# First weights in eight steps with the rows of x, four columns side by side, and squares of two rows at once

## The chip, the cores and the metric

The kernel runs on one core of one Trainium2 chip. The metric is the device time of one execution in microseconds (us), lower is better. Before the change the median of 3 runs is 984.67 us (984.04 to 986.51).

## What is computed

Two layers of a decoder trunk on 256 tokens of width 1024, in float32. Each layer is a half-weighted SwiGLU feed-forward, a token mixer, a cross-attention to a memory of 256 tokens, and a second feed-forward; every part reads an RMS-normed x. What matters here is the very first part:

```python
def rmsnorm(x, g):
    x32 = x.astype(jnp.float32)
    y = x32 * lax.rsqrt(jnp.mean(x32 * x32, axis=-1, keepdims=True) + EPS)
    return y.astype(x.dtype) * g

def swiglu(x, w_gate, w_up, w_down):
    return (jax.nn.silu(x @ w_gate) * (x @ w_up)) @ w_down

x = x + 0.5 * swiglu(rmsnorm(x, ffn1_norm[l]), ffn1_w_gate[l], ffn1_w_up[l], ffn1_w_down[l])
```

w_gate and w_up are 1024 x 2816, w_down 2816 x 1024. The mixer of the first layer needs a bias per head, looked up in a small table (rel_bias), and one sink per head (ev_sinks).

## The kernel before, in words

x lies with its 1024 features on the partitions, as 8 row blocks (KT = 8) of 128 features x 256 tokens. Weights are cut into tiles of 128x128; the host lays the 2768 tiles out in the order in which they are used. `Stream` (line 51) loads them in chunks of 16 tiles (1 MB) through SP's queue into four buffers `raw`, and splits them in blocks of 8 tiles (`fill`, line 87): ScalarE rounds a block to a high part `whi` (line 99), VectorE takes the rest as a low part `wlo` (line 100). x is split alike, with the gain of the norm multiplied in (`normed_tile`, line 263: ScalarE line 267, VectorE line 268). A product of one tile with one row block, a pair in what follows, is two matmuls (`mm`, line 319): whi against both parts of x, 512 columns (line 322), and wlo against the high part, 256 columns (line 323).

The scale of the norm (one over the root mean square) is not needed for the products, only when their sums are evacuated. `squares` (line 272) sums the squares of x over the row blocks, on GpSimd for the first seven (lines 275, 279, 280), on ScalarE and VectorE for the last (lines 282, 283); `norm_scale` (line 285) has TensorE sum over partitions (line 291), GpSimd take the power, and TensorE spread the result (line 301).

The work around the change is the start. Lines 221 to 226 issue the first loads: vecs (all gains) on ScalarE's queue, and on SP's queue, in turn, five pieces of x and five pieces of the first two chunks, then the third chunk. Lines 236 to 240 warm up TensorE with WARM = 9 matmuls of the identity matrix, which GpSimd makes first. Lines 896 to 899 split x and the first 32 tiles, and `gates` (line 405) multiplies three columns of w_gate side by side, so that each row block of x that arrives gives work to three accumulators (24 tiles in all); then the columns follow one by one (`gate_up`, line 416). A gate or up sum is joined out of PSUM into a buffer `w1` (eight of them) by line 332 on ScalarE and line 333 on VectorE, and waits there for the norm's scale.

`make_bias` (line 717) loads the bias table, the sinks (one row repeated over 128 partitions, line 723) and a one-hot matrix with three DMAs on GpSimd's queue.

TensorE's program follows `Order`: a list of work items, each with a cost, and tasks that fall due at a time on the list's own clock (`pe.after(delay, fn, cost)`); the squares' sum over partitions is due at 2300 of that clock, behind `gates`. The order of the instructions on each engine is then set at build time by a list scheduler; an engine runs its list in order.

Of the kernel before, what the change touches and what calls it, by code (L numbers as in the profile page):

```python
# [31 lines left out]
NEG = -1e30  # L32
BUCKETS = 32
# [15 lines left out]


class Stream:


# [4 lines left out]

    def __init__(self, nc, pool, src):
        self.nc, self.pool, self.src = nc, pool, src  # L60
        self.order = []
        self.raw, self.split = {}, {}
        self.n_loaded = self.n_split = 0
        self.due = deque()
        self.n_due = 0
        self.fine = False

    def load(self, cuts=(0, CHUNK)):

        c = self.n_loaded  # L70
        t = self.raw[c] = self.pool.tile([P, CHUNK * P], F32, name="raw", bufs=4)
        self.n_loaded += 1
        for i, j in zip(cuts, cuts[1:]):
            self.nc.sync.dma_start(t[:, i * P:j * P], self.src[c][:, i * P:j * P])
            yield

    def _load_to(self, n):
        while self.n_loaded < min(n, NTILES // CHUNK):
            for _ in self.load():
                pass  # L80

# [4 lines left out]

    def fill(self, cuts=None):
        if not self.due:
            return
        cuts = cuts or ((0, BLK // 2, BLK) if self.fine else (0, BLK))  # L90
        b = self.due.popleft()
        c, o = divmod(b * BLK, CHUNK)
        self._load_to(c + 1)
        raw = self.raw[c][:, o * P:(o + BLK) * P]
        hi = self.pool.tile([P, BLK * P], F32R, name="whi", bufs=self.BUFS)
        lo = self.pool.tile([P, BLK * P], F32R, name="wlo", bufs=self.BUFS)
        for i, j in zip(cuts, cuts[1:]):
            at = slice(i * P, j * P)
            self.nc.scalar.activation(hi[:, at], raw[:, at], AF.Copy)  # L99
            self.nc.vector.tensor_tensor(lo[:, at], raw[:, at], hi[:, at].bitcast(F32), op=ALU.subtract)  # L100
# [91 lines left out]
def build(nc, tc, ctx, a):  # L192
    consts = ctx.enter_context(tc.tile_pool(name="consts", bufs=1))
    wpool = ctx.enter_context(tc.tile_pool(name="wpool", bufs=1))
    act = ctx.enter_context(tc.tile_pool(name="act", bufs=1))
# [3 lines left out]
    def acc_tile():  # L199
        return psum.tile([P, 512], F32, name="acc", bufs=4)  # L200
# [10 lines left out]
    def w2():  # L211
        return act.tile([P, 512], F32, name="w2", bufs=6)
# [19 lines left out]
    mhalf = consts.tile([P, 2], F32, name="mhalf")  # L232
    nc.gpsimd.memset(mhalf, -0.5)


    warm = act.tile([P, 2], F32, name="ms", bufs=2)
    nc.scalar.activation(warm, mhalf, AF.Silu)
# [25 lines left out]
    def normed_tile(n, k, src):  # L263

        g = col(n.key, k)
        n.x[k] = x2 = Split(act.tile([P, 2 * S], F32R, name=n.name, bufs=n.n_bufs))
        nc.scalar.activation(x2.hi, halves(src), AF.Copy, scale=g)
        nc.vector.scalar_tensor_tensor(x2.lo, halves(src), g, x2.hi.bitcast(F32), op0=ALU.mult, op1=ALU.subtract)  # L268
        if not n.ready:
# [131 lines left out]
    def ffn(which, layer, n, nxt, first=False, last=False):  # L401
# [3 lines left out]
        def gates():  # L405

            for f in range(3):
                cur[f, 0] = acc_tile()
            for k in range(KT):
                for f in range(3):  # L410
                    w = ws.take(f"{which}_w_gate", layer, k * P, f * P)
                    mm(cur[f, 0], w, n.x[k], k == 0, k == KT - 1)
            for f in range(3):
                cur[f, 0] = join(w1(), cur[f, 0])
# [41 lines left out]
        def down_tok():  # L456
# [32 lines left out]
            def evac_tok(u, at, ps):  # L489
# [227 lines left out]
    def make_bias():  # L717

        tab = consts.tile([BUCKETS + 1, 8], F32, name="tab")
        nc.gpsimd.dma_start(tab[:BUCKETS], a["rel_bias"])  # L720
        nc.gpsimd.memset(tab[BUCKETS:BUCKETS + 1], NEG)
        sinks = consts.tile([P, 8], F32, name="sinks")
        nc.gpsimd.dma_start(sinks, bass.AP(tensor=a["ev_sinks"].tensor, offset=a["ev_sinks"].offset, ap=[[0, P], [1, 8]]))
# [11 lines left out]
        return sinks  # L735

# [276 lines left out]
```

## Time and profile before

| | us |
|---|---|
| median of 3 runs | 984.67 |
| lowest, highest | 984.04, 986.51 |
| profiled execution, its own time | 984.22 |
| its span in the trace | 982.4 |
| TensorE busy in the span | 968.7 (99%) |
| VectorE, ScalarE, GpSimd busy | 757.3, 580.6, 146.9 |

How to read it: times within the trace are us from the start of the span. PE is TensorE's matmuls, PEld its weight loads, DVE VectorE, ACT ScalarE, POOL GpSimd, SP the engine that issues most DMAs; a q behind an engine's name is its instruction queue. Matmuls overlap, so two rows of PE may run at one time, and the busy times of rows that overlap are not added up. Behind a row, in brackets, stands the time that the engine was idle before it and what ended that idle time. The profiled execution took 1.8 us more than its span.

### The profile page before, as it was taken

What the parts mean: (1) busy time and instruction counts of PE and PEld (TensorE: products, weight loads), DVE (VectorE), ACT (ScalarE), POOL (GpSimd) and SP (SyncE); (2) the same over time, 40 slices, a digit from 0 to 9 for tenths busy, and PEclk for the clock granted to TensorE, in tenths of its full rate; (3) what the DMA queues carried; (4) which work ended last, traced back from release to release, by engine and by line L of the source; (5) the groups of instructions that cost most, each with busy time, mean ns of one, the idle gap of its engine ahead of it and who ended that gap; (6) DMA issues with size and microseconds to landing.
All of it is one profiled execution on the core that took longest, in us unless ns stands there. A gap on an engine that the chain in (4) does not pass through costs nothing.

```text
span 982.4 us, 16594 instructions
## 1 busy us (share of the span) xinstructions
PE 968.7 (99%) x6442; PEld 902.3 (92%) x6442; DVE 757.3 (77%) x1284; ACT 580.6 (59%) x1026; POOL 146.9 (15%) x160
## 2 busy tenths in 40 slices
PE   7999999999999999999999999999999999999997
PEld 6899999999999999999999999999999999999896
DVE  6888877799876988877778878777668678887653
ACT  6665654575556666664556666555665657666542
POOL 6104003201241400002210000121005050000010
PEclk9999999999999999999999999999999999999999
DMA  9796655556463465565555565566545526555531
GB/s 308 256 343 236 225 187 209 172 215 214 171 212 133 171 211 188 201 214 189 198 204 190 205 214 186 201 212 217 179 154 187 181 95 219 210 199 192 209 129 44
DMA packets 28415, 193.66 MB, mean 197 GB/s; under 512 B 3346, under 2 KB 3730, under 8 KB 5808
## 3 DMA queue, kind: packets, MB, share of 16 engines
q1 hardware_dynamic: 26928, 186.66, 54.7%
q0 software_dynamic: 976, 5.37, 1.7%
q8 instruction: 50, 0.82, 0.3%
q10 hardware_dynamic: 432, 0.57, 0.2%
q14 instruction: 29, 0.24, 0.1%
HBM read 191.51 MB, written 4.22 MB: 199 GB/s over the span
## 4 chain that ended last, share of the span: by engine, by line
PE 97%; DMA 1%; SPq 0%; ACT 0%; DVE 0%; issue 0%; POOLq 0%; DVEq 0%
PE acc L322 41%; PE acc L323 21%; PE acc L327 7%; PE acc L329 7%; PE acc L328 7%; PE acc L481 1%; PE acc L482 1%; PE acc L480 1%; PE acc L370 1%; PE acc L371 1%; PE acc L372 1%; DMA raw<-in_w 1%; PE tr L587 1%; PE sc L571 1%; PE tr L579 1%; PE sc L480 0%
## 5 line engine op out<-in xcount | busy, mean ns | idle before, releaser
L100 DVE TENSOR_TENSOR wlo<-raw,whi 128x1024 fp32r<-128x1024 f32 (+2 forms) x356 | 435.1, 1225 | 150.8 <-ACT whi L99 147.9
L99 ACT ACTIVATE whi<-raw 128x1024 fp32r<-128x1024 f32 (+2 forms) x356 | 366.4, 1033 | 297.6 <-PE acc L322 137.0
L322 PE MATMUL acc<-x,whi 128*128 128x512 f32 x1408 | 462.7, 383 | 2.7 <-DVE x L268 2.7
L323 PE MATMUL acc<-x,wlo 128*128 128x256 f32 x1408 | 382.8, 273 | 0.5 <-DVE wlo L100 0.5
L322 PEld LDWEIGHTS acc<-x,whi 128*128 128x128 f32 x1408 | 265.9, 189 | 40.3 <-DVE x L268 3.3
L323 PEld LDWEIGHTS acc<-x,wlo 128*128 128x128 f32 x1408 | 269.9, 192 | 1.9 <-DVE wlo L100 1.5
L322 PE MATMUL acc<-h,whi 128*128 128x512 f32 x462 | 151.3, 382 | 0.0
L323 PE MATMUL acc<-h,wlo 128*128 128x256 f32 x462 | 125.4, 273 | 0.0
L322 PEld LDWEIGHTS acc<-h,whi 128*128 128x128 f32 x462 | 87.1, 189 | 12.0
L323 PEld LDWEIGHTS acc<-h,wlo 128*128 128x128 f32 x462 | 88.7, 192 | 0.2
L328 PE MATMUL acc<-h,whi 128*128 128x256 f32 x322 | 88.3, 278 | 0.0
L329 PE MATMUL acc<-h,wlo 128*128 128x256 f32 x322 | 87.5, 276 | 0.0
L327 PE MATMUL acc<-h,whi 128*128 128x256 f32 x322 | 86.3, 279 | 0.9 <-ACT h L386 0.9
L329 PE MATMUL acc<-x,wlo 128*128 128x256 f32 x304 | 84.6, 280 | 0.0
L328 PE MATMUL acc<-x,whi 128*128 128x256 f32 x304 | 83.5, 276 | 0.0
L327 PE MATMUL acc<-x,whi 128*128 128x256 f32 x304 | 82.7, 278 | 0.0
L333 DVE TENSOR_TENSOR w<-acc,w 128x256 f32<-128x256 f32 x197 | 82.2, 418 | 0.3
L332 ACT ACTIVATE w<-acc 128x256 f32<-128x256 f32 x197 | 72.6, 369 | 3.8 <-PE acc L323 3.8
L275 POOL TENSOR_TENSOR sqacc<-x 128x256 f32<-128x256 f32 x8 | 4.9, 615 | 421.4 <-DVE x L381 421.4
L279 POOL TENSOR_TENSOR sq<-x 128x256 f32<-128x256 f32 x48 | 53.1, 1112 | 89.5 <-DVE x L381 69.9
L327 PEld LDWEIGHTS acc<-h,whi 128*128 128x128 f32 x322 | 60.3, 192 | 2.0 <-ACT h L386 1.8
L329 PEld LDWEIGHTS acc<-h,wlo 128*128 128x128 f32 x322 | 61.7, 192 | 0.1
(179 smaller groups left out, 1207.1 us busy)
## 6 DMA issues: line engine op xcount, KB each, us to landing
raw<-in_w SPq DMA_DIRECT2D x171, 1024.0 KB, 5.0
dists<-line POOLq DMA_DIRECT2D x2, 1536.0 KB, 12.6
raw<-in_memT SPq DMA_DIRECT2D x3, 1024.0 KB, 4.9
bias<-dists POOLq DMA_DIRECT2D x2, 1024.0 KB, 10.1
raw<-in_w SPq DMA_DIRECT2D x2, 512.0 KB, 8.6
x<-in_xT SPq DMA_DIRECT2D x3, 256.0 KB, 8.3
kT<-in_final_norm SPq DMA_DIRECT2D x1, 512.0 KB, 3.7
out<-bias ACTq DMA_DIRECT2D x2, 256.0 KB, 2.7
```

The source lines that it names most:

```text
L99: self.nc.scalar.activation(hi[:, at], raw[:, at], AF.Copy)
L100: self.nc.vector.tensor_tensor(lo[:, at], raw[:, at], hi[:, at].bitcast(F32), op=ALU.subtract)
L279: nc.gpsimd.tensor_tensor(sq, src, src, op=ALU.mult)
L322: nc.tensor.matmul(ps, w[0], x2.both, start=start, stop=False)
L323: nc.tensor.matmul(ps[:, :S], w[1], x2.high, start=False, stop=stop)
L327: nc.tensor.matmul(ps[:, :S], w[0], x2.high, start=start, stop=False)
L328: nc.tensor.matmul(ps[:, :S], w[0], x2.low, start=False, stop=False)
L329: nc.tensor.matmul(ps[:, :S], w[1], x2.high, start=False, stop=stop)
L332: nc.scalar.activation(halves(out), unpaired(ps[:, S:]), AF.Copy)
L333: nc.vector.tensor_tensor(halves(out), unpaired(ps[:, :S]), halves(out), op=ALU.add)
L370: nc.tensor.matmul(ps[t], xh, wh, start=k == 0, stop=False)
L371: nc.tensor.matmul(ps[t], xh, wl, start=False, stop=False)
```

## The change

The first 32 tiles (FIRST = KT * SIDE, four columns of w_gate) leave the stream of 1 MB chunks. The host packs each row block of x with the four tiles that meet it into one row of 768 columns (`w0`, 8 x 128 x 768, 393 KB each), and SP loads these eight rows first, the first two of them in two pieces; two rows share one of the four `raw` buffers. The first norm reads x from these rows. Only the later work needs the tile x itself: it is loaded whole (1 MB) afterwards, and a GpSimd copy of one column makes that load wait for the fourth row's block. The squares leave the loop: ScalarE squares two row blocks at a time, from the tile x, GpSimd adds the four results, VectorE adds the two halves. They are due at 12000 of the order's clock and the sum over partitions at 18200. The warm-up uses a zero tile that VectorE clears, and 8 matmuls in place of 9. The bias table and the sinks become columns of vecs (84 to 100 columns), so that two of GpSimd's DMAs go; the load of the one-hot matrix is made to wait for x.

```diff
-WARM = 9
+WARM = 8
+SIDE = 4
+FIRST = KT * SIDE
+STEP = S + SIDE * P
-NVEC = VCOL["conv"] + 3 * 4
+VCOL["table"] = VCOL["conv"] + 3 * 4
+VCOL["sinks"] = VCOL["table"] + 8
+NVEC = VCOL["sinks"] + 8
...
+    def load_first(self):
+        rows = []
+        for k in range(KT):
+            if k % 2 == 0:
+                t = self.raw[k // 2] = self._raw()
+            o = k % 2 * STEP
+            cuts = {0: (0, S + P, STEP), 1: (0, S, STEP)}.get(k, (0, STEP))
+            for i, j in zip(cuts, cuts[1:]):
+                self.nc.sync.dma_start(t[:, o + i:o + j], self.first[k][:, i:j])
+            rows.append(t[:, o:o + S])
+        return rows
...
-    ws = Stream(nc, wpool, a["w"])
+    warm = consts.tile([P, P], F32, name="warm")
+    nc.vector.memset(warm, 0.0)
+    ws = Stream(nc, wpool, a["w0"], a["w"])
     nc.scalar.dma_start(vecs, a["vecs"])
-    pieces = chain(ws.load((0, 3, 9, CHUNK)), ws.load((0, 8, CHUNK)))
-    for k, n in ((0, 1), (1, 1), (2, 2), (4, 2), (6, 2)):
-        nc.sync.dma_start(x[:, k:k + n], a["xT"][:, k:k + n])
-        next(pieces)
-    ws._load_to(ws.AHEAD_CHUNKS)
+    first_rows = ws.load_first()
+    ws._load_to(ws.n_loaded + 1)
...
-        nc.tensor.matmul(pt[:, :P], ident, ident, start=True, stop=True)
+        nc.tensor.matmul(pt[:, :P], warm, warm, start=True, stop=True)
...
+    def squares_of_x(n):
+        two = None
+        for k in range(0, KT, 2):
+            sq = w2()
+            nc.scalar.activation(sq, x[:, k:k + 2].rearrange("p k s -> p (k s)"), AF.Square)
+            if two is None:
+                two = sq
+            else:
+                nc.gpsimd.tensor_tensor(two, two, sq, op=ALU.add)
+        n.acc = act.tile([P, S], F32, name="sqacc", bufs=2)
+        nc.vector.tensor_tensor(n.acc, two[:, :S], two[:, S:], op=ALU.add)
...
-            for f in range(3):
-                cur[f, 0] = acc_tile()
+            for f in range(SIDE):
+                cur[f, 0] = (acc_tile if f < SIDE // 2 else sc_tile)()
...
-        norm_scale(n)
+        if first:
+            pe.after(12000, lambda: squares_of_x(n), 0)
+        norm_scale(n, 18200 if first else 2300)
...
-        tab = consts.tile([BUCKETS + 1, 8], F32, name="tab")
-        nc.gpsimd.dma_start(tab[:BUCKETS], a["rel_bias"])
-        nc.gpsimd.memset(tab[BUCKETS:BUCKETS + 1], NEG)
-        sinks = consts.tile([P, 8], F32, name="sinks")
-        nc.gpsimd.dma_start(sinks, bass.AP(tensor=a["ev_sinks"].tensor, offset=a["ev_sinks"].offset, ap=[[0, P], [1, 8]]))
         oh = act.tile([BUCKETS + 1, 768], F32, name="bias", bufs=1)
+        nc.gpsimd.tensor_copy(oh[:, :1], x[:BUCKETS + 1, 0, :1])
         nc.gpsimd.dma_start(oh, a["onehot"])
...
+    n.acc = False
     for k in range(KT):
-        normed_tile(n, k, x[:, k])
+        normed_tile(n, k, first_rows[k])
         if k % 2 == 0:
-            ws.fill(((0, 3, 6, BLK), (0, 1, 4, BLK), (0, BLK), (0, BLK))[k // 2])
+            block = ws.begin()
+        cuts = (0, 1, SIDE) if k == 0 else (0, SIDE)
+        for i, j in zip(cuts, cuts[1:]):
+            ws.piece(block, k % 2 * SIDE + i, k % 2 * SIDE + j)
+        if k == KT // 2 - 1:
+            nc.gpsimd.tensor_copy(x[:, 0, :1], block[1][:, :1].bitcast(F32))
+            nc.sync.dma_start(x, a["xT"])
+    ws._load_to(ws.n_loaded + 1)
```

## Rows read from the trace of the kernel before

**Rows 1.** The waits of TensorE over the whole span: who waited for whom, us in total, times, the longest.
```profile
PE acc L322 <- DVE x L268: 2.7, 3, 1.3
PE tr L240 <- POOL ident masks.py:199: 2.5, 1, 2.5
PE acc L327 <- ACT h L386: 0.9, 2, 0.5
PE acc L323 <- DVE wlo L100: 0.5, 1, 0.5
```

**Rows 2.** TensorE's matmuls in order of time, the first 22 us: start, us, engine, line, operation, out<-in, count, and in brackets the idle time before.
```profile
2.54 4.21 PE L240 MATMUL tr<-ident 128*128 128x128 f32 x18 [2.54 <-POOL ident masks.py:199]
6.40 1.28 PE L322 MATMUL acc<-x,whi 128*128 128x512 f32 x3
7.85 0.81 PE L322 MATMUL acc<-x,whi 128*128 128x512 f32 x3
...
10.30 0.48 PE L322 MATMUL acc<-x,whi 128*128 128x512 f32 x1 [1.31 <-DVE x L268]
...
13.96 0.48 PE L322 MATMUL acc<-x,whi 128*128 128x512 f32 x1 [1.17 <-DVE x L268]
...
19.32 0.38 PE L322 MATMUL acc<-x,whi 128*128 128x512 f32 x1
19.68 0.38 PE L323 MATMUL acc<-x,wlo 128*128 128x256 f32 x1
19.89 0.38 PE L322 MATMUL acc<-x,whi 128*128 128x512 f32 x1
20.11 0.27 PE L323 MATMUL acc<-x,wlo 128*128 128x256 f32 x1
...
21.86 0.38 PE L322 MATMUL acc<-x,whi 128*128 128x512 f32 x1
22.07 0.50 PE L291 MATMUL tr<-ones,sqacc 128*128 128x1 f32 x4
```

**Rows 3.** Stretches of the start: from:to and length, busy us (and instructions) of PE, PEld, DVE, ACT and POOL, granted TensorE clock, mean busy share of the 16 DMA engines, GB/s.
```profile
2.00:3.40 1.40, 0.86 (x4) 0.86 (x5) 0.00 (x0) 0.68 (x2) 1.25 (x5) 1.00 0.93 240
3.40:5.50 2.10, 2.10 (x12) 2.10 (x12) 1.06 (x2) 1.30 (x3) 1.45 (x5) 1.00 0.74 272
5.50:7.60 2.10, 2.10 (x10) 1.96 (x10) 1.39 (x3) 1.04 (x4) 0.22 (x1) 1.00 1.05 175
7.60:10.00 2.40, 1.39 (x10) 1.12 (x8) 0.97 (x4) 0.89 (x3) 0.73 (x2) 1.00 0.98 331
10.00:13.00 3.00, 2.48 (x12) 1.80 (x12) 2.80 (x4) 2.09 (x5) 2.92 (x4) 1.00 1.05 393
```

**Rows 4.** DMA queues from 5.5 to 7.6 us: packets, MB, share of the 16 engines' time. q0 carries GpSimd's DMAs, q1 SP's.
```profile
q0 software_dynamic: 28, 0.00, 53.3%
q1 hardware_dynamic: 168, 0.36, 51.3%
```

**Rows 5.** GpSimd's list in order of time, the issues of its DMAs among it.
```profile
2.59 0.60 POOL L723 DMA_DIRECT2D sinks<-in_ev_sinks  x1
...
17.63 2.58 POOL L280 TENSOR_TENSOR sqacc<-sqacc,sq 128x256 f32<-128x256 f32 x2
```

**Rows 6.** DMA issues of the first 30 us: size of each, median us from issue to landing.
```profile
raw<-in_w SPq DMA_DIRECT2D x2, 512.0 KB, 8.6
x<-in_xT SPq DMA_DIRECT2D x3, 256.0 KB, 8.3
...
vecs<-in_vecs ACTq DMA_DIRECT2D x1, 42.0 KB, 2.6
...
sinks<-in_ev_sinks POOLq DMA_DIRECT2D x1, 4.0 KB, 6.2
```

**Rows 7.** The instructions that write or read the row blocks of x and the sum of squares: count, ns shortest/median/longest, first and last start.
```profile
L267 ACT ACTIVATE x<-x,vecs x8: 492/494/510, 3.4 to 14.6; 128x256 fp32r<-128x256 f32 x8
L268 DVE SCALAR_TENSOR_TENSOR x<-x,vecs x8: 473/829/953, 4.0 to 17.1; 128x256 fp32r<-128x256 f32 x8
L280 POOL TENSOR_TENSOR sqacc<-sqacc,sq x6: 794/910/1595, 9.8 to 18.6; 128x256 f32<-128x256 f32 x6
```

**Rows 8.** Groups of the first 22 us by line and shape: count, busy us, mean ns of one, idle time before.
```profile
L99 ACT ACTIVATE whi<-raw 128x512 fp32r<-128x512 f32 x1 | 0.6, 621 | 0.0
L99 ACT ACTIVATE whi<-raw 128x128 fp32r<-128x128 f32 x1 | 0.3, 292 | 0.0
L100 DVE TENSOR_TENSOR wlo<-raw,whi 128x512 fp32r<-128x512 f32 x1 | 1.1, 1096 | 0.0
L283 DVE TENSOR_TENSOR sqacc<-sqacc,sq 128x256 f32<-128x256 f32 x1 | 0.4, 427 | 0.6 <-POOL sqacc L280 0.6
masks.py:197 POOL MEMSET ident<- 128x128 f32 x1 | 0.2, 205 | 0.3 <-POOLq L979 0.3
```

**Rows 9.** Groups between 20 and 60 us by line and shape, columns as in rows 8.
```profile
L100 DVE TENSOR_TENSOR wlo<-raw,whi 128x1024 fp32r<-128x1024 f32 x18 | 21.7, 1221 | 4.1 <-ACT whi L99 4.0
L99 ACT ACTIVATE whi<-raw 128x1024 fp32r<-128x1024 f32 x18 | 18.9, 1061 | 10.4 <-PE acc L322 5.9 <-issue 2.6 <-ACT h L386 1.9
L332 ACT ACTIVATE w<-acc 128x256 f32<-128x256 f32 x16 | 5.8, 372 | 0.0
```

**Rows 10.** ScalarE in order of time, the first 22 us.
```profile
3.41 0.51 ACT L267 ACTIVATE x<-x,vecs 128x256 fp32r<-128x256 f32 x1 [0.72 <-DMA vecs<-in_vecs]
4.71 0.52 ACT L99 ACTIVATE whi<-raw 128x384 fp32r<-128x384 f32 x1 [0.79 <-DMA raw<-in_w]
```

More of the change, by code (lines that the diff above doesn't have):

```diff
@@ L57, with __init__ @@
     BUFS = 5
-    def __init__(self, nc, pool, src):
-        self.nc, self.pool, self.src = nc, pool, src
+    def __init__(self, nc, pool, first, src):
+        self.nc, self.pool, self.first, self.src = nc, pool, first, src
         self.order = []
         self.raw, self.split = {}, {}
-        self.n_loaded = self.n_split = 0
+        self.n_loaded = FIRST // BLK
+        self.n_split = 0
         self.due = deque()
@@ L66, in __init__, with _raw, chunk_of @@
         self.fine = False
[L68 to L75, printed above, removed]
-    def _load_to(self, n):
-        while self.n_loaded < min(n, NTILES // CHUNK):
-            for _ in self.load():
-                pass
+    def _raw(self):
+        return self.pool.tile([P, CHUNK * P], F32, name="raw", bufs=4)
+    def load_first(self):
[9 more added lines that the diff above has]
+        return rows
+    def chunk_of(self, b):
+        if b * BLK < FIRST:
+            return b, (S, STEP + S)
+        c, o = divmod(b * BLK - FIRST, CHUNK)
+        return FIRST // BLK + c, (o * P, (o + BLK // 2) * P)
+    def _load_to(self, n):
+        while self.n_loaded < min(n, FIRST // BLK + (NTILES - FIRST) // CHUNK):
+            c = self.n_loaded
+            t = self.raw[c] = self._raw()
+            self.nc.sync.dma_start(t, self.src[c - FIRST // BLK])
+            self.n_loaded += 1
     def _due_to(self, n):
@@ L85, in _due_to, with begin @@
             self.n_due += 1
[L87 to L90, printed above, removed]
+    def begin(self):
         b = self.due.popleft()
-        c, o = divmod(b * BLK, CHUNK)
+        c, (left, right) = self.chunk_of(b)
         self._load_to(c + 1)
-        raw = self.raw[c][:, o * P:(o + BLK) * P]
         hi = self.pool.tile([P, BLK * P], F32R, name="whi", bufs=self.BUFS)
         lo = self.pool.tile([P, BLK * P], F32R, name="wlo", bufs=self.BUFS)
[L97 to L100, printed above, removed]
         self.split[b] = (hi, lo)
@@ L103, in fill, with piece @@
         self.n_split = b + 1
+        return hi, lo, self.raw[c], left, right
+    def piece(self, block, i, j):
+        hi, lo, raw, left, right = block
+        o = left + i * P if i < BLK // 2 else right + (i - BLK // 2) * P
+        src, at = raw[:, o:o + (j - i) * P], slice(i * P, j * P)
+        self.nc.scalar.activation(hi[:, at], src, AF.Copy)
+        self.nc.vector.tensor_tensor(lo[:, at], src, hi[:, at].bitcast(F32), op=ALU.subtract)
+    def fill(self):
+        if not self.due:
+            return
+        block = self.begin()
+        cuts = (0, BLK // 2, BLK) if self.fine else (0, BLK)
+        for i, j in zip(cuts, cuts[1:]):
+            self.piece(block, i, j)
     def flush(self):
@@ L233, in build @@
     nc.gpsimd.memset(mhalf, -0.5)
-    warm = act.tile([P, 2], F32, name="ms", bufs=2)
-    nc.scalar.activation(warm, mhalf, AF.Silu)
+    nc.scalar.activation(act.tile([P, 2], F32, name="ms", bufs=2), warm[:, :2], AF.Silu)
     pt = tr_tile()
     for _ in range(WARM):
-        nc.tensor.matmul(pt[:, :P], ident, ident, start=True, stop=True)
+        nc.tensor.matmul(pt[:, :P], warm, warm, start=True, stop=True)
     pe = Order()
@@ L268, in normed_tile @@
         nc.vector.scalar_tensor_tensor(x2.lo, halves(src), g, x2.hi.bitcast(F32), op0=ALU.mult, op1=ALU.subtract)
-        if not n.ready:
+        if n.acc is not False and not n.ready:
             squares(n, k, src)
@@ L405, in gates @@
         def gates():
-            for f in range(3):
-                cur[f, 0] = acc_tile()
+            for f in range(SIDE):
+                cur[f, 0] = (acc_tile if f < SIDE // 2 else sc_tile)()
             for k in range(KT):
-                for f in range(3):
+                for f in range(SIDE):
                     w = ws.take(f"{which}_w_gate", layer, k * P, f * P)
                     mm(cur[f, 0], w, n.x[k], k == 0, k == KT - 1)
-            for f in range(3):
+            for f in range(SIDE):
                 cur[f, 0] = join(w1(), cur[f, 0])
@@ L514, in down_tok @@
                 part(range(FT - late), *right)] + [part(end, reg) for reg in right]
-        norm_scale(n)
+        if first:
+            pe.after(12000, lambda: squares_of_x(n), 0)
+        norm_scale(n, 18200 if first else 2300)
         parts = (range(4), range(4, KT))
-        ups = [(always, gates, 3 * KT * 327)] if first else []
+        ups = [(always, gates, FIRST * 327)] if first else []
         ups += [gate_up(f, part, ks) for f in range(FT) for part in range(2) for ks in parts
-                if not (first and part == 0 and f < 3)]
+                if not (first and part == 0 and f < SIDE)]
         if last:
@@ L717, in make_bias @@
     def make_bias():
[L719 to L723 removed]
         oh = act.tile([BUCKETS + 1, 768], F32, name="bias", bufs=1)
+        nc.gpsimd.tensor_copy(oh[:, :1], x[:BUCKETS + 1, 0, :1])
         nc.gpsimd.dma_start(oh, a["onehot"])
+        tab = vecs[:BUCKETS + 1, VCOL["table"]:VCOL["table"] + 8]
         by = act.tile([8, 768], F32, name="kT", bufs=2)
@@ L904, in biases @@
     def biases():
-        early["sinks"] = make_bias()
+        make_bias()
         early["bias"] = load_bias(0)
@@ L923, in build @@
     ffn("ffn1", 0, n, nxt, first=True)
-    bias, sinks = early["bias"], early["sinks"]
+    bias, sinks = early["bias"], vecs[:, VCOL["sinks"]:VCOL["sinks"] + 8]
     kv = {}
@@ L979 @@
     nc = bacc.Bacc("TRN2", target_bir_lowering=False, num_devices=1)
-    shapes = {"w": (NTILES // CHUNK, P, CHUNK * P), "xT": (P, KT, S), "memT": (P, KT, S), "vecs": (P, NVEC), "final_norm": (1, D),
-              "rel_bias": (BUCKETS, 8), "ev_sinks": (1, 8), "onehot": (BUCKETS + 1, 768)}
+    shapes = {"w0": (KT, P, STEP), "w": ((NTILES - FIRST) // CHUNK, P, CHUNK * P), "xT": (P, KT, S), "memT": (P, KT, S), "vecs": (P, NVEC), "final_norm": (1, D),
+              "onehot": (BUCKETS + 1, 768)}
     a = {k: nc.dram_tensor(f"in_{k}", s, F32, kind="ExternalInput").ap() for k, s in shapes.items()}
@@ L993 @@
     w["ev_w_out"] = inp["ev_w_out"][:, rows]
-    stream = np.empty((NTILES // CHUNK, P, CHUNK, P), inp["x"].dtype)
+    xT = tokens_last(inp["x"][0])
+    first = np.empty((KT, P, STEP), inp["x"].dtype)
+    first[:, :, :S] = xT.transpose(1, 0, 2)
+    stream = np.empty(((NTILES - FIRST) // CHUNK, P, CHUNK, P), inp["x"].dtype)
     for i, (name, layer, r, c, step) in enumerate(order):
-        stream[i // CHUNK, :, i % CHUNK] = w[name][layer, r:r + P, c:c + P * step:step]
+        t = w[name][layer, r:r + P, c:c + P * step:step]
+        if i < FIRST:
+            o = S + i % SIDE * P
+            first[i // SIDE, :, o:o + P] = t
+        else:
+            stream[(i - FIRST) // CHUNK, :, (i - FIRST) % CHUNK] = t
     vecs = [inp[n][l].reshape(KT, P) for n in NORMS for l in range(DEPTH)]
@@ L1000 @@
     vecs += [inp["ev_conv_w"][0].reshape(12, P)]
+    table = np.zeros((P, 8), inp["x"].dtype)
+    table[:BUCKETS], table[BUCKETS] = inp["rel_bias"], NEG
+    sinks = np.repeat(inp["ev_sinks"][:1], P, axis=0)
     arrays = {
+        "w0": first,
         "w": stream.reshape(shapes["w"]),
-        "xT": tokens_last(inp["x"][0]),
+        "xT": xT,
         "memT": tokens_last(inp["mem"][0]),
-        "vecs": np.ascontiguousarray(np.concatenate(vecs).T),
+        "vecs": np.ascontiguousarray(np.concatenate([np.concatenate(vecs).T, table, sinks], axis=1)),
         "final_norm": inp["final_norm"].reshape(1, D),
-        "rel_bias": np.ascontiguousarray(inp["rel_bias"]),
-        "ev_sinks": np.ascontiguousarray(inp["ev_sinks"]),
         "onehot": onehot(),
```

4 lines of the change are left out of this document (2 added, 2 removed).

## The prediction

> **What bounds the kernel now.** Read the waits of TensorE over the whole span first [rows 1]: four kinds of wait, 6.6 us in all, against 968.7 us busy. The engine is full. Apart from 0.9 us on h, every recorded wait is on the identity, on x or on wlo. TensorE in order of time [rows 2] shows where: 2.54 us ahead of the warm-up, gaps of 1.31 and 1.17 us while x and the first weights trickle in, and the last one ahead of the wlo product at 19.68. From 19.89 on pairs follow without a hole, one per 0.328 us ((21.86 - 19.89) / 6, from the row of the sixth pair after it). The pair at 19.89 is the 26th (24 of the gates, two after), so the start costs as much as if TensorE had begun dense work at 19.89 - 25 x 0.328 = 11.7 us. Only this 11.7 us can shrink: what follows is TensorE's own work, and the change leaves its amount alone.
>
> Why so late? The stretches [rows 3] show the transfers: 240 and 272 GB/s at first, then a hole with 175 GB/s between 5.5 and 7.6 us, then 331, and 393 at last. The hole has a cause in the queues of that stretch [rows 4]: GpSimd's queue moved 0.00 MB in 28 packets and held 53.3% of the sixteen DMA engines' time. It is the sinks, 4 KB repeated over 128 partitions, issued at 2.59 and landed 6.2 us later [rows 5, 6]. And VectorE's share of each row block is stretched while GpSimd squares beside it: 829 ns at the median for the low part of x, where the shortest takes 473 [rows 7], and 1096 for half a block of wlo [rows 8], where a whole block takes 1221 between 20 and 60 us [rows 9].
>
> **The change, part by part.** My yardstick is the start of the 33rd pair, the first that needs the ordinary stream in the new kernel. Before, without the sums, it would stand at 19.89 + 7 x 0.328 = 22.2 us.
>
> *Warm-up.* It no longer waits for GpSimd's identity. VectorE's clearing of a 128x128 tile does not occur in the trace; GpSimd's takes 205 ns [rows 8]. I take a start at 1.0 us (bounds 0.8 and 2.5), and the 16 matmul rows of eight warm-ups take 16 / 18 of 6.40 - 2.54, from the old warm-up's first row to the first pair [rows 2]: 3.4 us, end 4.4 us.
>
> *First pair.* ScalarE could begin on x at 3.41, when vecs had landed [rows 10]; vecs grows from 84 to 100 columns, 19%, which I bound by 0 and 0.2 us. High part of x 0.49, low part 0.47 without GpSimd beside it [rows 7], one tile of whi (0.29 [rows 8]) meanwhile: first pair at about 4.6.
>
> *Rows of x with weights.* SP issues as many loads as before (ten pieces, then a chunk). A row is 128 x 768 x 4 bytes, 0.393 MB; with vecs the eight are 3.20 MB. By 5.5 us the old kernel had moved 1.4 x 0.240 + 2.1 x 0.272 = 0.91 MB; I keep that, and take the 393 GB/s of the last stretch from then on, since the sinks are gone. Landing lags moving: the first three loads (0.37 MB) were moved at 3.53 by those rates, and ScalarE got the last of them at 4.71 [rows 10], so 1.2 us at most; the lower bound is 0.6, half of it. The second piece of row 0 (0.44 MB in all) lands at 5.0, row 1 (0.84 MB) at 6.4, row 2 at 7.5, then one per 1.0 us, row 7 at 12.5.
>
> *Pace.* Per row TensorE needs 4 x 0.328 = 1.31 us. ScalarE needs 0.49 + 0.62 = 1.11, VectorE 0.47 for x and 0.61 for wlo (half of 1221), 1.08. The 1.10 us that GpSimd's presence would give for that half block (1096) makes it 1.57 and would bound; but the squares have gone from here. So from row 1 on TensorE is the bound: row 1 can start at 6.4 + 0.62 = 7.1 with its weights, I take 7.2; seven rows take 9.2, and gates end at 16.4. Ends: 15.1 if the second piece and row 1 land with the short lag at the full rate (4.6 + 32 x 0.328); 17.9 if rows 0 and 1 go at the pace of the three matmuls at 6.40 (0.43 us each instead of 0.27 in the next row [rows 2], the lower of TensorE's two clock levels, 1.2 GHz, though the recorded grant is 1.00 there): row 1 then starts at 7.4, takes 2.6, and six rows follow.
>
> *The next weights.* Chunk 4 waits on SP's queue until the first raw buffer is free (row 1 split, about 7.8 us), which is ahead of its turn; behind it queue x whole and chunk 5. By 393 GB/s chunk 4 (4.25 MB in all) is moved at 14.0 and landed at 15.2, whi at 16.2, wlo at 17.4, 0.8 us after the first wlo product could run. Chunk 5 comes behind x (6.34 MB): landed at 20.5, wlo at 22.8, where TensorE wants it at 16.4 + 16 x 0.328 + 0.2 = 21.9 (0.2 is the step from a pair's first matmul at 19.89 to its second at 20.11 [rows 2]). These two are one lateness, not a sum: 0 to 1.0 us, I take 0.5. The reload of x costs 2.7 us of transfers here and is covered but for that; without the cover it would be the whole 2.7.
>
> *Squares.* Removed: seven squares and six adds on GpSimd, one square on ScalarE. Added: four squares 128x512 on ScalarE (no such row; the copy of that width takes 0.62 [rows 8], so 2.5 us in all; by copies of 256 and 1024 columns, 0.49 [rows 7] and 1.06 [rows 9], between 2.0 and 4.2), three adds of 512 columns on GpSimd, 0.43 us on VectorE [rows 8]. They wait for x whole, landed at 17.9 at the latest by the sum above; behind them on ScalarE's list stand the next whi and the joins (0.37 each [rows 9]). ScalarE has 5.4 us between 16.2 and 21.6 for one whi, five joins and the squares, 5.4: just enough. An add of 256 columns took 794 to 1595 ns [rows 7], so one of 512 between 0.8 and 3.2. From the second square (19.1) on, three adds and VectorE's end the sum at 22 to 29. TensorE's sums stand on the list at 18200, behind 56 pairs: 16.9 + 24 x 0.328 = 24.8. At the median (1.8 each) the sum is ready at 25.0: I take 0.2 us of waiting, bounds 0 and 4.3. Before, the sums at 22.07 came without a wait [rows 2].
>
> *Elsewhere.* Two DMAs on GpSimd go. GpSimd's copy ahead of the one-hot load waits for x, with only work behind it that is due later. The wait at h is not touched.
>
> *Sum.* 22.2 - 16.4 - 0.5 - 0.2 = 5.1 us. The profiled execution took 984.22, so 979.1; it lies 0.45 below the median of 984.67, against which I state the forecast: **979.6**.
>
> **The rivals.** *The sums wait* (0.19). TensorE's list is in order, so a late sum of squares stops every pair behind it. For it: late in the old start two adds took 2.58 us [rows 5], so a wide one may take 2.6, and the sum would be ready at 27.3, 2.5 us behind its place; the gain shrinks to 22.2 - 16.4 - 0.5 - 2.5 = 2.8, 981.9; with the longest adds to 1.0, 983.7. Against it: GpSimd will have nothing else to do, and the list leaves more time than the old one did.
>
> *The change doesn't do what it says* (0.11): the rows do not arrive faster, because the slow start is not the sinks but the many small loads. For it: 240 and 272 GB/s before the hole. What decides is the rate from 4.4 us on, where row 0's 0.44 MB should be there (moved at 3.8, with the short lag). Chunk 4 needs 3.80 MB more; its last wlo is 2.3 us behind its landing. No gain if that is at 22.4, as the old 33rd pair's would be, so at 3.80 / (20.1 - 4.4) = 242 GB/s; at 175 GB/s it is at 4.4 + 21.7 + 2.3 = 28.4, 6.0 us late: **slower**, 990.7. Over 0.3% slower starts at 3.80 / (23.1 - 4.4) = 203 GB/s. Against it: between 10 and 13 us the queue mostly carried pieces of 256 and 512 KB, and moved 393 GB/s [rows 3, 6].
>
> The Trainium skill speaks for this rival (DMA: Bandwidth & Descriptors, Bandwidth): transfers should be batched to 1 MB and more for three quarters of the peak rate, and by the fit in its section on the anatomy of one DMA each costs 2.0 us beside its bytes. Ten first loads one after another would by that estimate take 10 x 2.0 + 3.2 / 0.436 = 27 us, and the gates would end near 30, which gives 992. The stretch at 393 GB/s disagrees: queued pieces share that fixed part.
>
> **How the numbers follow.** A measurement of this kernel tells 0.3%, 2.95 us, from no change. Forecast 0.70: from 22.2 - 15.1 = 7.1 us gained (977.6) to 22.2 - 17.9 - 1.0 = 3.3 (981.4). The sums' wait 0.19, half of it still above 2.95 us gained. The slow rows 0.11: 0.06 slower, 0.05 within 0.3%. Faster 0.70 + 0.09 = 0.79, within 0.15, slower 0.06. The range takes in the forecast and the cheaper two thirds of the sums' wait: 977.6 to 982.8.
>
> **What would show it.** Right: no hole between 5.5 and 7.6 us, and GpSimd's queue near nothing there; the low parts of x at 473 ns instead of 829; eight rows of TensorE at 1.31 us each; the 33rd pair at 16 to 17.5; the sums without a wait. Wrong: TensorE waiting at the sums for VectorE's add (first rival), rows further apart than 1.31 us with ScalarE waiting for DMA (second), or a wait after the gates for whi or wlo of more than 1 us.

## The result and the profile after

The changed kernel takes 979.62 us at the median (979.29 to 979.72, 4 runs), the kernel before 984.95 beside it (984.04 to 986.51, 4 runs): a ratio of 0.9944, interval 0.9926 to 0.9961. The profiled execution took 979.29 us with a span of 977.2, against 984.22 and 982.4. The kernel before spreads more: of its 31 executions beside the first four experiments, the 14 with a mean granted TensorE clock of 0.997 or less have a median of 986.4, the 17 with 0.998 or 0.999 one of 985.2, while the changed kernel's four all have 0.998 or 0.999.

The waits of TensorE over the whole span, after, columns as in [rows 1]:
```profile
PE tr L271 <- DVE warm L254: 1.1, 1, 1.1
PE acc L371 <- ACT h L430: 0.9, 2, 0.5
PE acc L367 <- DVE wlo L128: 0.5, 1, 0.5
PE acc L366 <- ACT whi L127: 0.4, 1, 0.4
```
The 2.7 us for x and 1.4 of the 2.5 us ahead of the warm-up are gone; a new wait of 0.4 us is for whi. TensorE in order of time, the answer to [rows 2]:
```profile
1.06 3.78 PE L271 MATMUL tr<-warm 128*128 128x128 f32 x16 [1.06 <-DVE warm L254]
4.65 0.63 PE L366 MATMUL acc<-x,whi 128*128 128x512 f32 x1
...
6.80 0.70 PE L366 MATMUL acc<-x,whi 128*128 128x512 f32 x2 [0.43 <-ACT whi L127]
...
8.23 0.67 PE L366 MATMUL acc<-x,whi 128*128 128x512 f32 x2
...
9.62 0.60 PE L366 MATMUL acc<-x,whi 128*128 128x512 f32 x2
...
14.86 0.60 PE L366 MATMUL acc<-x,whi 128*128 128x512 f32 x2
...
16.17 0.94 PE L366 MATMUL acc<-x,whi 128*128 128x512 f32 x2
16.95 0.36 PE L367 MATMUL acc<-x,wlo 128*128 128x256 f32 x1
...
21.84 0.61 PE L366 MATMUL acc<-x,whi 128*128 128x512 f32 x2
22.92 0.38 PE L367 MATMUL acc<-x,wlo 128*128 128x256 f32 x1 [0.48 <-DVE wlo L128]
...
27.39 0.50 PE L335 MATMUL tr<-ones,sqacc 128*128 128x1 f32 x4
```
The rows of x begin at 4.65, 6.80, 8.23, 9.62 and then every 1.31 us; the 33rd pair stands at 16.17, where the yardstick of before was 22.2. Counted on by the whi matmuls of the pairs, the 501st pair starts at 173.53 us, before at 178.36: the 4.8 us that the start gave are still there.

Stretches, columns and bounds as in [rows 3], and the queues from 5.5 to 7.6 us as in [rows 4]:
```profile
2.00:3.40 1.40, 1.40 (x9) 1.40 (x8) 0.00 (x0) 0.70 (x3) 0.00 (x0) 1.00 0.91 300
3.40:5.50 2.10, 2.10 (x11) 1.95 (x11) 1.26 (x3) 1.14 (x4) 0.00 (x0) 1.00 0.87 209
5.50:7.60 2.10, 1.67 (x10) 1.35 (x9) 1.18 (x2) 1.62 (x4) 0.00 (x0) 1.00 1.03 405
7.60:10.00 2.40, 2.40 (x16) 2.22 (x15) 2.35 (x5) 2.33 (x5) 0.37 (x1) 1.00 1.03 414
10.00:13.00 3.00, 3.00 (x19) 2.73 (x19) 3.00 (x7) 3.00 (x7) 0.00 (x0) 1.00 1.05 431
```
```profile
q1 hardware_dynamic: 313, 0.85, 103.4%
```
The hole at 5.5 us is filled, 405 GB/s instead of 175, and GpSimd's queue is absent from it. Another low stretch stays ahead of it: 209 GB/s.

VectorE's part of each row of x, as in [rows 7], and its list behind the gates, with GpSimd's adds and ScalarE's squares of the same time:
```profile
L299 DVE SCALAR_TENSOR_TENSOR x<-raw,vecs,x x8: 475/478/485, 4.1 to 12.8; 128x256 fp32r<-128x256 f32 x8
```
```profile
15.65 2.36 DVE L128 TENSOR_TENSOR wlo<-raw,whi 128x1024 fp32r<-128x1024 f32 x2 [1.74 <-ACT whi L127]
...
21.05 1.81 DVE L128 TENSOR_TENSOR wlo<-raw,whi 128x1024 fp32r<-128x1024 f32 x1 [0.58 <-ACT whi L127]
22.79 2.30 DVE L128 TENSOR_TENSOR wlo<-raw,whi 128x1024 fp32r<-128x1024 f32 x1
25.01 0.41 DVE L327 TENSOR_TENSOR sqacc<-w 128x256 f32<-128x256 f32 x1
```
```profile
19.13 1.30 POOL L325 TENSOR_TENSOR w<-w,w 128x512 f32<-128x512 f32 x1
20.51 1.28 POOL L325 TENSOR_TENSOR w<-w,w 128x512 f32<-128x512 f32 x1
21.87 2.14 POOL L325 TENSOR_TENSOR w<-w,w 128x512 f32<-128x512 f32 x1
```
```profile
14.56 2.01 ACT L127 ACTIVATE whi<-raw 128x1024 fp32r<-128x1024 f32 x2 [1.45 <-DMA raw<-in_w]
...
17.53 2.21 ACT L321 ACTIVATE w<-x 128x512 f32<-128x512 f32 x4
...
19.92 1.99 ACT L127 ACTIVATE whi<-raw 128x1024 fp32r<-128x1024 f32 x2
```
All eight low parts take 475 to 485 ns. But the meeting of GpSimd and VectorE has moved: two blocks of wlo take 1.81 and 2.30 us beside the wide adds (4.03 us from the start of the first to the end of the second), where two take 2.36 without them.

### The profile page after: what moved, and what is told of

It is laid out like the page before. It is cut to its first block, busy times and chain, and to the rows that moved or that the text cites. A ratio compares the mean times of both kernels' runs of the same rounds, so it can differ in the third digit from the quotient of the medians.

```text
span 977.2 us, 16591 instructions
## 1 busy us (share of the span) xinstructions
PE 967.6 (99%) x6440; PEld 902.0 (92%) x6440; DVE 755.6 (77%) x1286; ACT 582.6 (60%) x1030; POOL 141.1 (14%) x149
## 4 chain that ended last, share of the span: by engine, by line
PE 97%; DMA 1%; ACT 1%; DVE 0%; issue 0%; SPq 0%; POOLq 0%; DVEq 0%
PE acc L366 41%; PE acc L367 20%; PE acc L371 7%; PE acc L373 7%; PE acc L372 7%; PE acc L526 1%; PE acc L525 1%; PE acc L524 1%; DMA raw<-in_w 1%; PE acc L414 1%; PE acc L415 1%; PE acc L416 1%; PE tr L633 1%; PE sc L617 1%; PE tr L625 1%; PE sc L524 0%
## 5 line engine op out<-in xcount | busy, mean ns | idle before, releaser
L366 PE MATMUL acc<-x,whi 128*128 128x512 f32 x1392 | 457.5, 383 | 0.5 <-ACT whi L127 0.4
L367 PE MATMUL acc<-x,wlo 128*128 128x256 f32 x1392 | 377.8, 273 | 0.5 <-DVE wlo L128 0.5
L366 PEld LDWEIGHTS acc<-x,whi 128*128 128x128 f32 x1392 | 262.3, 189 | 37.2 <-ACT whi L127 1.0
L367 PEld LDWEIGHTS acc<-x,wlo 128*128 128x128 f32 x1392 | 267.2, 192 | 1.6 <-DVE wlo L128 0.8
L366 PEld LDWEIGHTS acc<-h,whi 128*128 128x128 f32 x462 | 87.1, 189 | 11.9
L373 PE MATMUL acc<-x,wlo 128*128 128x256 f32 x304 | 84.6, 280 | 0.0
L371 PEld LDWEIGHTS acc<-h,whi 128*128 128x128 f32 x322 | 60.3, 192 | 2.0 <-ACT h L430 1.8
L372 PEld LDWEIGHTS acc<-h,whi 128*128 128x128 f32 x322 | 61.7, 192 | 0.1
```

What stands on the lines that cost most here:

```text
L366: nc.tensor.matmul(ps, w[0], x2.both, start=start, stop=False)
L367: nc.tensor.matmul(ps[:, :S], w[1], x2.high, start=False, stop=stop)
L371: nc.tensor.matmul(ps[:, :S], w[0], x2.high, start=start, stop=False)
L372: nc.tensor.matmul(ps[:, :S], w[0], x2.low, start=False, stop=False)
L373: nc.tensor.matmul(ps[:, :S], w[1], x2.high, start=False, stop=stop)
```

## The experiments

Theory: the gain is one of the start, made by three things in a line: transfers without the sinks' hole, VectorE without GpSimd's squares beside it, and four pairs for each row. The rivals: any one of them alone makes it; or the warm-up does. Four kernels do one or two parts on the kernel before, four undo one part of the changed kernel, three aim at what is left behind the gates, and one at the slow stretch ahead of 5.5 us. Times are compared with the kernel before in the same series; the position of a pair comes from one profiled execution each. The changed kernel itself did not run again in these series.

**b_no_sinks**: bias table and sinks as columns of vecs.
```diff
...
-        nc.gpsimd.dma_start(tab[:BUCKETS], a["rel_bias"])
...
-        nc.gpsimd.dma_start(sinks, bass.AP(tensor=a["ev_sinks"].tensor, offset=a["ev_sinks"].offset, ap=[[0, P], [1, 8]]))
+        tab = vecs[:BUCKETS + 1, VCOL["table"]:VCOL["table"] + 8]
+        sinks = vecs[:, VCOL["sinks"]:VCOL["sinks"] + 8]
...
```


> The kernel before, with the bias table and the sinks moved into vecs and nothing else. Theory A (the sinks' small packets hold the DMA engines between 5.5 and 7.6 us): that stretch moves 350 GB/s or more instead of 175, x and weights land about 1.2 us earlier; since GpSimd's squares still stretch VectorE's work, 0.5 to 1.2 us faster than before. Rival B (the hole belongs to the start with many loads, whoever issues them): the hole stays, within 0.3 us of before.

983.88 against 985.89 us, ratio 0.9981 (0.9972 to 0.9991). The stretch, and SP's queue in it:
```profile
5.50:7.60 2.10, 2.10 (x10) 1.92 (x9) 0.55 (x2) 1.07 (x3) 1.47 (x2) 1.00 0.95 265
```
```profile
q1 hardware_dynamic: 234, 0.56, 95.5%
```
265 GB/s instead of 175, less than the 350 of theory A, and the 33rd pair at 21.94 instead of 22.63. The sinks cost time by themselves, 2.0 us by the medians, above theory A's 0.5 to 1.2, and 0.7 by this trace; that many small loads are the whole cause falls. But the sinks are not the whole hole either: SP's queue fills the stretch to 95.5% and moves 0.56 MB in it, where the changed kernel's moves 0.85 MB at 103.4%. What makes that difference was not tested; the packed rows are one candidate.

**b_squares_late**: `squares_of_x` in the kernel before, due at 9400, sums at 15600.
```diff
...
+        if first:
+            pe.after(9400, lambda: squares_of_x(n), 0)
+        norm_scale(n, 15600 if first else 2300)
...
```


> The kernel before, with the squares of the first norm taken out of the loop: four squares of two row blocks on ScalarE, three adds on GpSimd, due behind the gates (9400 and 15600 of the order's clock). Theory A (GpSimd beside VectorE sets the pace of the split): low parts of x near 475 ns, 1.0 to 2.2 us faster. Rival B (the transfers set the pace, VectorE only fills the time): low parts near 475 ns too, but less than 0.5 us faster.

985.77 against 985.89, ratio 1.0002 (0.9992 to 1.0011): no change. The low parts of x and GpSimd's list:
```profile
L268 DVE SCALAR_TENSOR_TENSOR x<-x,vecs x8: 474/482/1500, 4.0 to 18.1; 128x256 fp32r<-128x256 f32 x8
```
```profile
11.54 1.28 POOL L294 TENSOR_TENSOR w<-w,w 128x512 f32<-128x512 f32 x1 [7.63 <-ACT w L290]
13.86 1.52 POOL L294 TENSOR_TENSOR w<-w,w 128x512 f32<-128x512 f32 x1 [1.04 <-ACT w L290]
16.12 1.79 POOL L294 TENSOR_TENSOR w<-w,w 128x512 f32<-128x512 f32 x1 [0.74 <-ACT w L290]
```
Both signs of rival B came, 482 ns at the median and no gain. Yet it is not the test that it was meant to be: squares and adds stand among the rows again, and one low part takes 1500 ns. My reading is that x was there, so the scheduler placed them early, and that in the changed kernel the late reload of x keeps them out (they begin at 17.5 there); no run separates the reload from the due times.

**b_sinks_and_squares**: the two edits above together.
```diff
...
-        nc.gpsimd.dma_start(tab[:BUCKETS], a["rel_bias"])
...
+            pe.after(9400, lambda: squares_of_x(n), 0)
...
```


> The kernel before with both edits, sinks in vecs and late squares. Theory A (two bounds, one behind the other): more than the sum of the two alone, 2.0 to 3.5 us faster, as each alone uncovers the other. Rival B (one of them alone is the bound): as much as the better of the two alone.

983.46 against 985.89, ratio 0.9983 (0.9973 to 0.9992): the better of the two alone, as rival B had it, though with the squares not late, this does not tell the theories apart.

**b_four_wide**: four columns side by side in the kernel before.
```diff
-            for f in range(3):
-                cur[f, 0] = acc_tile()
+            for f in range(4):
+                cur[f, 0] = (acc_tile if f < 2 else sc_tile)()
...
```


> The kernel before with four columns side by side instead of three, loads and squares as before. Theory A (TensorE's gaps between rows take the eight added pairs, 2.6 us of work): 1.0 to 2.2 us faster. Rival B (the fourth column's weights come no earlier, as the pieces are cut for three): less than 0.5 us faster or slower.

984.75 against 985.89, ratio 0.9991 (0.9981 to 1.0000). The profiled execution can't carry a reading: TensorE waited 2.44 us for x before 11.91, and from 13.5 us on its granted clock was 0.52, the lower of its two levels:
```profile
13.50:17.00 3.50, 3.21 (x11) 2.94 (x12) 3.50 (x5) 2.95 (x5) 3.42 (x5) 0.52 1.01 419
```
By the medians four columns alone are worth 1.1 us, by the interval between nothing and 1.9: the runs do not decide between A (1.0 to 2.2) and B (under 0.5).

**a_sinks_back**: the changed kernel with GpSimd's two DMAs again.
```diff
-        tab = vecs[:BUCKETS + 1, VCOL["table"]:VCOL["table"] + 8]
...
+        nc.gpsimd.dma_start(tab[:BUCKETS], a["rel_bias"])
...
+        nc.gpsimd.dma_start(early["sinks"], bass.AP(tensor=a["ev_sinks"].tensor, offset=a["ev_sinks"].offset, ap=[[0, P], [1, 8]]))
...
```


> The changed kernel with the bias table and the sinks loaded by GpSimd's DMAs again. Theory A (their small packets hold the DMA engines for about 1.2 us, and TensorE, dense from row 1 on, can't make up for it): rows 2 and 3 land 1 us later, the 33rd pair stands at 16.8 to 17.6 instead of 16.17, 0.5 to 1.4 us slower than the changed kernel. Rival B (the eight rows have enough lead): less than 0.4 us slower.

981.12 us against 984.27, ratio 0.9969 (0.9957 to 0.9981); a_identity_warm, in the same series, has 979.62. The stretch, its queues, and TensorE at the third row of x:
```profile
5.50:7.60 2.10, 1.70 (x9) 1.37 (x9) 1.18 (x2) 0.94 (x2) 0.00 (x0) 1.00 1.00 182
```
```profile
q1 hardware_dynamic: 143, 0.38, 50.5%
q0 software_dynamic: 21, 0.00, 49.5%
```
```profile
9.90 0.67 PE L366 MATMUL acc<-x,whi 128*128 128x512 f32 x2 [1.68 <-DVE x L299]
```
The hole is back with the queue that made it, that row starts at 9.90 instead of 8.23, and the 33rd pair stands at 17.84, just above the 17.6 that A gave at most. By the runs the sinks are worth 1.5 us against a_identity_warm, also just above A's range; the pair's position alone would not show that, since it varies by as much (last section).

**a_squares_in_loop**: the changed kernel, squares on GpSimd as the rows come.
```diff
-        if first:
-            pe.after(12000, lambda: squares_of_x(n), 0)
-        norm_scale(n, 18200 if first else 2300)
+        norm_scale(n)
...
-    n.acc = False
```


> The changed kernel with the squares back in the loop on GpSimd (line 272 of before, from the first rows), sum due at 2300; the reload of x stays. Theory A (with rows at 1.0 us, VectorE at 1.5 us a row beside GpSimd becomes the bound): the 33rd pair at 17.5 to 18.5, but no wait at the third block after the gates (the 0.48 us at 22.92 was made by GpSimd's wide adds); 0.7 to 2.0 us slower than the changed kernel. Rival B (squares are hidden either way): within 0.4 us.

981.47 against 984.27, ratio 0.9970 (0.9958 to 0.9981), 1.9 us over a_identity_warm. VectorE in the first 22 us, columns as in [rows 8]:
```profile
L128 DVE TENSOR_TENSOR wlo<-raw,whi 128x512 fp32r<-128x512 f32 x7 | 6.8, 971 | 0.7 <-ACT whi L127 0.7
L299 DVE SCALAR_TENSOR_TENSOR x<-raw,vecs,x 128x256 fp32r<-128x256 f32 x8 | 6.0, 748 | 1.2 <-ACT x L298 1.1
```
0.75 + 0.97 = 1.72 us a row, against TensorE's 1.31: VectorE is the bound, as A had it. The 33rd pair comes at 19.77, with the sums ahead of it; even without them (the step over the sums is 1.03 us instead of 0.33) it would stand at 19.1 at the earliest, later than A's 17.5 to 18.5. A also missed that the wait at the third block would go: 0.28 us for wlo stay, at 26.25, with no wide add of GpSimd near it. The loss of 1.9 us is inside A's range. Here the squares truly are put back among the rows, which b_squares_late did not take out.

**a_identity_warm**: nine warm-ups on the identity.
```diff
-WARM = 8
+WARM = 9
...
-        nc.tensor.matmul(pt[:, :P], warm, warm, start=True, stop=True)
+        nc.tensor.matmul(pt[:, :P], ident, ident, start=True, stop=True)
```


> The changed kernel with nine warm-ups on GpSimd's identity again. Theory A (row 1's transfer sets when dense work begins, the warm-up only fills the time ahead of it): first pair at about 5.2 instead of 4.65, rows from the second on unchanged within 0.3 us; total within 0.4 us. Rival B (warm-up and first pairs stand in one line): 0.5 to 0.9 us slower.

979.62 against 984.27, ratio 0.9953 (0.9938 to 0.9967). First pair at 5.28, third row at 8.59, 33rd pair at 16.52. The median is that of the changed kernel, but in another series; beside the kernel before, this one is 4.65 us faster and the changed one 5.33, with intervals that overlap. The rows from the second on are 0.35 to 0.45 us later than in the changed kernel, where theory A allowed 0.3; one execution each cannot tell so little.

This run also puts back only a part of the old warm-up. It starts here at 1.42, in the changed kernel at 1.06, in the kernel before at 2.54, because there GpSimd's list has the issue of the table's load ahead of the second step of the identity. First TensorE in this run, then GpSimd in the kernel before:
```profile
1.42 4.21 PE L271 MATMUL tr<-ident 128*128 128x128 f32 x18 [1.42 <-POOL cv L868]
```
```profile
1.37 0.70 POOL L720 DMA_DIRECT2D tab<-in_rel_bias  x1 [0.36 <-issue]
2.17 0.32 POOL masks.py:199 TENSOR_SCALAR_AFFINE_SELECT ident<-ident 128x128 f32<-128x128 f32 x1
```
So clearing a zero tile instead of using the identity shows no gain here. But most of the earlier warm-up, 1.1 of 1.5 us, comes with GpSimd's loads going, and what that part is worth was not tested: between the first and the 33rd pair of this run TensorE waits for nothing on record, so nothing there shows that the transfers would hide a start as late as before.

**a_three_wide**: eight rows, three columns side by side, the fourth behind them.
```diff
-            for f in range(SIDE):
-                cur[f, 0] = (acc_tile if f < SIDE // 2 else sc_tile)()
+            for f in range(3):
+                cur[f, 0] = acc_tile()
...
```


> The changed kernel with the same eight rows, but three columns side by side and the fourth behind them. Theory A (a row lands every 1.0 us, three pairs take 0.98, four 1.31: with three TensorE waits for rows now and then, and the eight pairs behind make it up only in part): 33rd pair at 16.3 to 17.2, 0.2 to 1.0 us slower. Rival B (without the four side by side, the gaps of the old start come back): 1.5 us slower or more.

980.43 against 984.27, ratio 0.9961 (0.9947 to 0.9975), 0.8 us over a_identity_warm, inside A's range, but not for A's reason. TensorE's longest wait:
```profile
PE acc L366 <- DVE w L377: 1.2, 1, 1.2
```
The fourth column ends later than the joins' place in VectorE's list allows: TensorE waits behind the gates (33rd pair at 18.49, outside A's 16.3 to 17.2) for an accumulator to be joined, and hardly between rows (0.3 us on record). So the 0.8 us are the price of the fourth column in this place, with its accumulator, not of gaps between rows.

**a_adds_vector**, **a_half_blocks**, **a_both**: what is left behind the gates; the first edit below, the second, and both.
```diff
-                nc.gpsimd.tensor_tensor(two, two, sq, op=ALU.add)
+                nc.vector.tensor_tensor(two, two, sq, op=ALU.add)
...
-        self.fine = False
+        self.fine = True
```


> The changed kernel with the three wide adds of squares on VectorE instead of GpSimd. Theory A (the two blocks of wlo behind 21.05 took 4.03 us instead of 2.36 because GpSimd was adding beside them, and that made the wait of 0.48 us at 22.92): blocks of wlo at 1.2 us each, the wait gone or under 0.15 us, 0.3 to 0.8 us faster than the changed kernel. Rival B (chunk 5, queued behind the reload of x, comes too late): the wait stays at 0.4 us or more, within 0.2 us.

> The changed kernel with blocks of weights split in halves (four tiles at a time) from the start until the first norm is scaled. Theory A (at the 33rd pair TensorE waits for a whole block of wlo, 1.2 us, of which it needs one tile): 0.43 us lost there shrink below 0.15, the wait at 22.92 by about 0.5; 0.4 to 0.9 us faster. Rival B (ScalarE and VectorE pay for twice the instructions): within 0.2 us or slower.

> The changed kernel with adds on VectorE and blocks in halves. Theory A (both waits behind the gates go): 0.7 to 1.2 us faster than the changed kernel, below 979. Rival B (the two edits cure the same wait): as fast as the better of the two alone.

980.28, 980.33 and 978.72 us against 985.88: ratios 0.9943 (0.9928 to 0.9958), 0.9944 (0.9928 to 0.9961), 0.9930 (0.9915 to 0.9944). The loads up to the gates' end are the same program in all of them, yet the 33rd pair stands at 17.67, 17.41 and 16.85, so I compare from there to the 501st: 157.36 us in the changed kernel, 157.18, 156.87 and 156.57 in these (a later 33rd pair shortens it by itself: 157.04 in a_sinks_back). The adds alone give at most the 0.2 us of that comparison, and the wait for wlo stays at 0.41: the figures of rival B. In that kernel, ScalarE, VectorE and TensorE:
```profile
21.30 1.99 ACT L127 ACTIVATE whi<-raw 128x1024 fp32r<-128x1024 f32 x2
```
```profile
22.37 0.68 DVE L325 TENSOR_TENSOR w<-w,w 128x512 f32<-128x512 f32 x1
22.97 1.22 DVE L128 TENSOR_TENSOR wlo<-raw,whi 128x1024 fp32r<-128x1024 f32 x1
```
```profile
24.24 0.38 PE L367 MATMUL acc<-x,wlo 128*128 128x256 f32 x1 [0.41 <-DVE wlo L128]
```
wlo takes 1.22 us again, but begins later, behind VectorE's own adds; and whi begins behind the squares on ScalarE, without a wait for a transfer. So neither theory's cause holds: not only GpSimd's presence, and not chunk 5. The block is late because squares, adds and joins stand ahead of it on two lists, and TensorE needs one tile of it at once. With halves alone the loss at the first block is gone (33rd to 42nd pair in 2.95 us, as without a hole), 0.27 us of waiting stay at the third block, and the ratio is that of the changed kernel. With both edits no wait for wlo is left, and the stretch is 0.8 us shorter; a_both has the lowest median of all. Its runs (978.55 to 979.01, 4) lie below all those of its two halves in the same series (979.19 to 980.67, 8); from the changed kernel, which ran in another, the intervals of the ratios don't tell it apart.

**a_vecs_512**: vecs filled up to 128 columns.
```diff
-NVEC = VCOL["sinks"] + 8
+NVEC = 128
...
```


> The changed kernel with vecs filled up to 128 columns, 512 bytes a partition instead of 400. Theory A (the stretch of 209 GB/s between 3.4 and 5.5 us comes from vecs' short pieces): that stretch moves 300 GB/s or more, row 1 lands 0.5 us earlier, its wait of 0.43 us goes, 0.3 to 0.5 us faster. Rival B (that hole has another cause): the stretch stays under 250 GB/s, no change in time.

980.19 against 985.88, ratio 0.9947 (0.9933 to 0.9962). The stretch:
```profile
3.40:5.50 2.10, 1.77 (x11) 1.52 (x11) 1.30 (x3) 1.20 (x4) 0.00 (x0) 1.00 0.77 200
```
200 GB/s, as rival B had it: vecs' short pieces are not the cause. What makes this stretch slow stays open; over the variants of the changed kernel it moves 180 to 239 GB/s.

## Why the prediction was right

Point by point, for the profiled execution. *Warm-up*: start 1.06, forecast 1.0; first pair 4.65, forecast 4.6. *Transfers*: the hole filled; 405 GB/s from 5.5 on where 393 was taken. *Pace*: 1.31 us a row; VectorE 478 ns and 0.69 a row, ScalarE 0.51 and 0.61, both under it. *33rd pair*: 16.17, forecast 16.4. *Squares*: 2.21 us on ScalarE (2.5), 1.63 an add on GpSimd (1.8). *The sums*: no wait, forecast 0.2. This step was off in its working, and came out by luck: the scheduler put the sums behind 63 pairs, not 56, at 27.39, and the sum of squares was there at 25.42. Behind 56 pairs, where the 57th pair stands at 25.10, it would have been 0.3 us late. The first rival fell with it. *The slow rows*: fell; queued pieces of 384 KB moved at 405 to 431 GB/s. The fit of 2.0 us for each DMA that this rival took from the Trainium skill (DMA: Bandwidth & Descriptors, Anatomy of one DMA) is given there for DMAs that GpSimd issues; these loads are SP's.

The term that was mis-sized is the lateness behind the gates: 0.5 us taken, 1.0 the upper bound, 1.2 found. By the pairs' positions, 0.43 at the first block (from 16.17 to the 42nd pair at 19.55 there are 3.38 us, nine steps of 0.328 make 2.95) and 0.75 from there over the third block (to the 58th pair at 25.54 there are 5.99 us, sixteen steps make 5.24). The step that failed is that these two would be one lateness and not a sum: they add up. The first is the one priced for chunk 4: ScalarE waits for the transfer until 14.56 (forecast 15.2), and wlo is ready 0.5 us after the first wlo product could run (forecast 0.8). The second was priced as chunk 5 behind the reload of x, but that chunk was in time: ScalarE takes it at 19.92 without a wait for a transfer, behind squares and joins. With 1.22 us for wlo, the block that VectorE begins at 21.05 would be ready at 22.27, 0.2 us after its first product could run (22.06, a step of 0.22 behind 21.84); beside GpSimd's adds it takes 1.81. I had priced that meeting only in the rows. The errors (0.2 better at the gates, 0.7 worse behind them, 0.2 better at the sums) nearly cancel, which is luck: 4.9 us by the profiled executions where 5.1 was forecast. That the median of 979.62 meets the forecast of 979.6 so closely is luck too. The medians' 5.3 owe the rest to the spread of the kernel before, which goes in part with its mean granted clock; where in an execution the clock falls, only the profile of b_four_wide shows.

Two readings in the prediction do not stand. No idle time is on record ahead of the wlo product at 19.68; the last recorded waits in the start of the kernel before are 0.54 us for wlo before 16.50 and 0.26 for x before 17.25. The dense work from 19.89 on, which the sum rests on, is right. And the upper end of the range called the slow pace of the first three matmuls the lower clock level: the granted clock is 1.00 in every stretch shown of both kernels up to 13 us, so no run shows that. In the changed kernel row 1 began at 6.80, ahead of the 7.2 taken.

Where the gain is: undone one at a time, and against a_identity_warm of the same series, the sinks are worth 1.5 us, the squares 1.9, the fourth column 0.8: together 4.2, where a_identity_warm is 4.65 faster than the kernel before. That they add up is not shown. All runs of these three in that series lie above those of a_identity_warm: 979.47 to 979.99 for a_identity_warm (4 runs), 980.28 to 980.55 for a_three_wide (5), 980.64 to 982.06 for a_sinks_back (6), 981.23 to 981.64 for a_squares_in_loop (6). Each of them, undone, leaves most of the gain, so no single one makes it. On the kernel before, by the medians, the sinks gave 2.0, the fourth column 1.1 and the squares nothing, since they did not move. The warm-up on a zero tile is worth nothing that the runs show; the earlier start of GpSimd's identity, and what packing a row of x with its weights is worth by itself, were not measured.

## What to carry to other kernels

Price an early DMA by the time its packets hold the engines, not by its bytes: 4 KB repeated over 128 partitions held them as long as 0.36 MB of x and weights beside it (53.3 and 51.3% of the stretch). Undo each part of a change from the finished version as well as adding it to the old one: the squares would not move in the old kernel, and only the undoing priced them. Look also at what an undone part does not bring back: the identity had come late behind a load that another part of the change removed. Work that is taken off one stage lands beside another: look what it meets there, and whether the built program has it where it was meant to be.

## What the runs showed of the hardware

The same program up to the gates' end put the 33rd pair at 16.17, 17.67, 17.41 and 16.85 us in four profiled executions (after, a_adds_vector, a_half_blocks, a_both): the first loads' landing varies by more than most edits are worth. A wide add on GpSimd takes 1.28 us in b_squares_late and 1.27 in b_sinks_and_squares at the least. In the changed kernel the add that lies wholly beside wlo takes 2.14, and the two blocks of wlo 1.81 and 2.30 instead of 1.22: both lose. In b_four_wide TensorE waited 2.44 us before 11.91, and its granted clock was 0.52 from 13.5 to 17 us, where the kernel before has 1.00.
